# Weights packed by the host in tile order, and one ring of six 8 KB buffers for weights and modulations, in a seven-part network on one core

## The chip, the cores and the metric

The kernel runs on one core of one Trainium2 chip. The metric is the device time of one execution in microseconds. What the host does to the inputs before the launch is not in it. Three runs of the kernel before took 1244.87, 1247.49 and 1250.49 us (median 1247.49).

## The reference

The reference is a network on `x` of 256 tokens by 1024 features, in float32, with seven parts in a row: mixer ab, feed-forward, mixer cd, feed-forward (the first block), feed-forward, convolution and state space mixer, feed-forward (the second block). Cut to the frame:

```python
def first_block(...):
    for layer in range(2):
        shift, scale, gate = split(c @ mod_w[layer, 0] + mod_b[layer, 0], 3)
        h = rms_norm(x, norm_w[layer, 0, 0]) * (1 + scale) + shift
        y = mixer_ab(h, ...) if layer % 2 == 0 else mixer_cd(h, ...)
        x = x + gate * rms_norm(y, norm_w[layer, 0, 1])
        ... # the same with swiglu(h, ffn_w_in[layer], ffn_w_out[layer])
def swiglu(h, w_in, w_out):
    gate, up = split(h @ w_in, 2)
    return (silu(gate) * up) @ w_out          # 1024 -> 2 x 2816 -> 1024
```

Each mixer is a projection of `h` by a matrix of 1024 rows, attention in several kinds over heads of 64 features (in the second block a short convolution and a state space model), and an output projection of 1024 by 1024. Each part needs three modulation vectors of 1024 (shift, scale, gate), each a product of one condition vector with a matrix of 1024 by 1024; that makes 21, the first two of which are made at the start.

## The kernel before, in words

**Products.** A float32 product is made of three passes (`mm3`, L106 to L108): a weight tile that has come from DRAM as `raw` is split by ScalarE into a high part (`whi`, L184) and by VectorE into a low part (`wlo`, L185), each in a ring of four tiles. Where the other operand is one piece, the raw tile goes to TensorE as it is (L104, L447). TensorE's order is the program's; the other engines and the DMA issues are ordered by a scheduler that simulates the timeline. All loads are issued by SP, one after the other: an issue that has to wait for its buffer holds those behind it.

**Weights.** `raw()` gives tiles of 8 KB per partition in a ring of four. `load_cols` (L198) takes columns of a matrix of 1024 rows: for 256 columns it is one load of 1 MB in rows of 1 KB, for pairs of 128 columns two loads of 512 KB in rows of 512 B. `load_rows` (L206) takes 512 rows. `tok_items` (L783) loads `ab_v`, three column ranges for each of two halves, so six loads. `load_q` (L721) loads the queries of the two groups apart. `loads_perm` (L941) loads the output weights of the two attention mixers in the order of the heads: two loads of 64 partitions each for one tile, rows of 4 KB. The feed-forward part (`ffn`) takes a step per 256 columns of gate and up (two tiles, four splits), then eleven tiles of the down matrix (L587). A mixer's `finish` calls `ahead`, which loads the first weights of the part that follows.

**Modulations.** `mod_start` clears an accumulator (POOL, L242), loads the bias into its first row (4 KB, L243), and then in eight pieces loads 1024 numbers per partition (`mraw`, 4 KB rows, a ring of four of its own, L250) and adds them, scaled, on VectorE (L252). `mod_end` sums over the partitions with two products (L276, L277). This work is queued in the background (`bg`, `pay`) and called between the steps of each part, for a later part.

```python
r = self.wp.tile([128, D], F32, tag="mraw", name="mraw", bufs=4)
nc.sync.dma_start(out=r, in_=wv[:, kk, :])
with self.behind(kk == 0):
    nc.vector.scalar_tensor_tensor(acc, r, c[:, kk:kk + 1], acc, ALU.mult, ALU.add)
```

**The first two modulations** (`start`, L1612) come in loads of 512 KB, rows of 2 KB, in quarters, summed on TensorE (L1616) and VectorE (L1619).

**Small loads.** The relative bias is written to DRAM (`rd`) and read back as tiles T, four loads of 32 partitions each (`bias_load`, L828); in the first mixer the copy out of T at L1016 comes before the softmax of later heads (L611, L618) on VectorE. The position embeddings (`setup`, L1695) are turned by TensorE at L1697. L1003 spreads the compressed values.

**Order in time** in the profile: start to some 40 us, mixer ab to 187, feed-forward to 384, mixer cd to 513, feed-forward to 714 and 905, the third mixer to 1049, the last feed-forward to the end.

Of the kernel before, what the change touches and what calls it, by code (L numbers as in the profile page):

```python
# [27 lines left out]
# per part of the network: weight tiles kept split beyond the ring's, modulations made early (and where),  # L28
# budgets and lags of the background work, parts with a second accumulator
# [4 lines left out]
ACC2 = (1, 3, 4)  # L34
E_F32 = 2.7182817459106445
# [3 lines left out]
def shape_constants(np):  # L39
# [20 lines left out]
    return c, oh, m  # L60


class Net:
# [74 lines left out]
    def plan(self, slots):  # L138
        """the waiting work, by its time, over steps of the given slack"""
# [51 lines left out]
    def load_cols(self, w, cols):  # L191
        """[1024, n] columns (a list of (start, stop)) -> raw [128, 8, total]"""
        tot = sum(b - a for a, b in cols)
        r = self.raw()
        v = r[:, :8 * tot].rearrange("p (k n) -> p k n", k=8)
        o = 0
        for a, b in cols:
            self.nc.sync.dma_start(out=v[:, :, o:o + b - a],  # L198
                                   in_=w[:, a:b].rearrange("(k p) n -> p k n", p=128))
            o += b - a  # L200
        return v

    def load_rows(self, w, r0, c0, c1):
        """rows r0 .. r0 + 511 of some columns -> raw [128, 4, n]"""
        r = self.raw()[:, :4 * (c1 - c0)].rearrange("p (k n) -> p k n", k=4)
        self.nc.sync.dma_start(out=r, in_=w[r0:r0 + 512, c0:c1].rearrange("(k p) n -> p k n", p=128))  # L206
        return r
# [6 lines left out]
    def chain(items, ahead=1):  # L214
        """items (prepare, run): closures that prepare `ahead` items beyond their own"""
# [9 lines left out]
    def proj_a(self, w, xh, xl):  # L225
        """weights [128, 8, 128] stationary -> psum [128 features, 256 tokens]"""
# [6 lines left out]
    # ---------------------------------------------------------------- mods  # L233
    def mod_start(self, w, b, c, grain):
        """b + c @ w, as partial sums over 128 partitions"""
# [7 lines left out]
        nc.sync.dma_start(out=acc[0:1, :], in_=b)  # L243
        wv = w.rearrange("(p k) n -> p k n", p=128)

        def piece(i):
# [7 lines left out]
        return acc, [piece(i) for i in range(8 // grain)]  # L254

    def behind(self, on):
        """behind the last part's norm on the vector engine"""
# [12 lines left out]
    def mod_end(self, b, part, kind, arg, dst):  # L270
        """sum over partitions, for all partitions: dst [128, 1024]"""
# [13 lines left out]
    def mod(self, key, w, b, c, kind, arg, row=None, grain=2):  # L285
        """queue the work on one modulation vector; the result is self.m[key]"""
        box = {}

        def start():
            box["acc"], box["pieces"] = self.mod_start(w, b, c, grain)  # L290
# [46 lines left out]
    def mean_sq(self, srcs, n):  # L337
        """two halves of rows [128, 512] -> their parts of the mean square"""
# [6 lines left out]
    def norm_ew(self, h, ws, sh):  # L345
        """token-major rms_norm(x) * ws + sh, rows of half h: two tiles of 512 columns"""
# [13 lines left out]
    def norm_tr(self, h, ts, hh, hl):  # L360
        """into feature-major hi and lo parts"""
# [12 lines left out]
    def post_norm(self, h, ys, gw):  # L374
        """x += rms_norm(y) * gw, rows of half h"""
# [17 lines left out]
    def boundary(self, s):  # L393
        """what follows the output projection of part s: -> ew(h, ys), tr(h)"""
# [43 lines left out]
    # ---------------------------------------------------------------- dense  # L438
# [14 lines left out]
    def out_items(self, ys, halves, loads, ks, nk, xh, xl, keep=None, pool=None):  # L453
        """items for two k-tiles each; loads(i, raw) fills raw [128, 2, 1024] with the rows of two k-tiles"""
        def prepare(i):
            r = self.raw().rearrange("p (k n) -> p k n", k=2)
            loads(i, r)
# [28 lines left out]
    def ahead(self, n=2):  # L486
        """the next part's first weights; self.first() is to hand them over"""
        s, I = self.s + 1, self.I
        if s == 5:
            us = [self.load_cols(I["w_in_2"][0], [(1536 + 256 * i, 1792 + 256 * i)]) for i in range(2)]  # L490
            self.first = lambda: us
        elif s == 2:
            rs = [self.load_rows(I["w_in_cd"][0], 512 * i, 1792, 2304) for i in range(2)]
            self.split_ahead([(r[:, 2 * i:2 * i + 2, :], [2, 512]) for r in rs for i in range(2)], n)
        elif s < 7:
            rs = [self.load_cols(w, [(0, 256)]) for w in self.ffn_weights(s)[:2]]
# [11 lines left out]
    def ffn_weights(self, s):  # L508
        I = self.I
        if s < 4:  # L510
            w = I["ffn_w_in"][s // 2]
            return w[:, :DFF], w[:, DFF:], I["ffn_w_out"][s // 2]
        n = "ffn1" if s == 4 else "ffn2"
        return I[n + "_w_gate_2"][0], I[n + "_w_up_2"][0], I[n + "_w_down_2"][0]

    def out_halves(self, loads, nk, xh, xl, s):
        """the output projection, the last four k-tiles half of the rows after half"""
# [3 lines left out]
        items = self.out_items(ys, (0, 1), loads, range(joint), nk, xh, xl)  # L521
        items += self.out_items(ys, (0,), loads, range(joint, nk // 2), nk, xh, xl, kept, self.fp)
# [21 lines left out]
    def ffn(self, s, wg, wu, wd, hh, hl):  # L544
        nc = self.nc
        with self.tc.tile_pool(name="ffn", bufs=1) as fp:
# [10 lines left out]
            # the first columns token-major: half 0 before half 1 is there  # L557
# [13 lines left out]
            for c in range(1, NF // 2):  # L571
                rg = self.load_cols(wg, [(256 * c, 256 * c + 256)])
                ru = self.load_cols(wu, [(256 * c, 256 * c + 256)])
                for j in range(2):
# [9 lines left out]
                    self.pay(WP)  # L584

            def loads(i, r):
# [1229 lines left out]
```

## Time and profile before

| | |
|---|---|
| median of three runs | 1247.49 us |
| span of the profiled execution | 1248.2 us |
| mean granted TensorE clock in it | 0.980 |
| TensorE busy | 1177.6 us |
| VectorE busy | 919.5 us |
| ScalarE busy | 611.5 us |
| moved by DMA | 304.38 MB, 244 GB/s |
| share of the 16 DMA engines | 74.7% |

The span runs from the first to the last instruction of the execution that was profiled; the page has no other time of that execution. A busy time is the union of an engine's instructions. In the rows, "x4" says that four instructions were merged, and what stands in square brackets or behind the bar is the engine's idle time before, with the instruction or load that ended it. The DMA share of a stretch is a mean over the 16 engines; it can come out a little over 1. The granted clock is 1 at 2.4 GHz and 0.5 at 1.2 GHz.

### The profile page before, as it was taken

What the parts mean: (1) busy time and instruction counts of PE and PEld (TensorE: products, weight loads), DVE (VectorE), ACT (ScalarE), POOL (GpSimd) and SP (SyncE); (2) the same over time, 40 slices, a digit from 0 to 9 for tenths busy, and PEclk for the clock granted to TensorE, in tenths of its full rate; (3) what the DMA queues carried; (4) which work ended last, traced back from release to release, by engine and by line L of the source; (5) the groups of instructions that cost most, each with busy time, mean ns of one, the idle gap of its engine ahead of it and who ended that gap; (6) DMA issues with size and microseconds to landing.
All of it is one profiled execution on the core that took longest, in us unless ns stands there. A gap on an engine that the chain in (4) does not pass through costs nothing.

```text
span 1248.2 us, 19610 instructions
## 1 busy us (share of the span) xinstructions
PE 1177.6 (94%) x7475; PEld 1019.2 (82%) x7475; DVE 919.5 (74%) x1378; ACT 611.5 (49%) x1110; POOL 136.9 (11%) x182
## 2 busy tenths in 40 slices
PE   6897999999999969899999989999999979999997
PEld 2795658999887955699998789998888747999986
DVE  6786839877758677796985699789559978755545
ACT  2364635445444645454454546776642423544433
POOL 2000000000001003100100010000007951000000
PEclk9997999999999989999999999999999989999999
DMA  9999498968965979798887479789665465755540
GB/s 341 309 277 274 121 283 277 355 211 298 349 227 154 271 242 232 247 342 296 295 314 264 161 242 353 244 314 364 230 201 152 154 211 168 227 165 183 203 169 34
DMA packets 203629, 304.38 MB, mean 244 GB/s; under 512 B 18423, under 2 KB 153331, under 8 KB 203534
## 3 DMA queue, kind: packets, MB, share of 16 engines
q1 hardware_dynamic: 203534, 303.12, 74.7%
q8 instruction: 59, 0.97, 0.3%
q14 instruction: 36, 0.29, 0.1%
HBM read 295.97 MB, written 7.11 MB: 243 GB/s over the span
## 4 chain that ended last, share of the span: by engine, by line
PE 35%; issue 17%; DVE 6%; POOL 3%; ACT 2%; DMA 1%; POOLq 0%; SPq 0%; DVEq 0%; ACTq 0%
PE ps L108 6%; PE ps L106 6%; PE ps L107 6%; PE y L451 3%; PE y L449 3%; PE y L450 3%; PE y L447 2%; PE tok L480 1%; PE ps L1360 1%; DVE st L1412 1%; DVE wlo L185 1%; PE glu L1529 1%; POOL xt L1404 1%; DVE ue L1080 1%; PE ps L365 1%
## 5 line engine op out<-in xcount | busy, mean ns | idle before, releaser
L184 ACT ACTIVATE whi<-raw 128x1024 fp32r<-128x1024 f32 (+2 forms) x308 | 318.4, 1042 | 398.5 <-PE ps L107 158.2
L185 DVE TENSOR_TENSOR wlo<-raw,whi 128x1024 fp32r<-128x1024 f32 (+2 forms) x308 | 368.6, 1204 | 179.1 <-ACT whi L184 178.4
L106 PE MATMUL ps<-hhi,whi 128*128 128x256 f32 x1488 | 424.7, 285 | 1.5 <-DVE st L611 1.5
L108 PE MATMUL ps<-hhi,wlo 128*128 128x256 f32 x1488 | 422.3, 284 | 4.0 <-DVE wlo L185 4.0
L107 PE MATMUL ps<-hlo,whi 128*128 128x256 f32 x1488 | 421.9, 284 | 0.0
L108 PEld LDWEIGHTS ps<-hhi,wlo 128*128 128x128 f32 x1488 | 286.3, 192 | 5.1 <-DVE wlo L185 5.1
L106 PEld LDWEIGHTS ps<-hhi,whi 128*128 128x128 f32 x1488 | 286.3, 192 | 4.2 <-DVE st L611 1.7
L107 PEld LDWEIGHTS ps<-hlo,whi 128*128 128x128 f32 x1488 | 286.4, 192 | 1.4 <-DVE wlo L185 0.5
L252 DVE SCALAR_TENSOR_TENSOR macc<-mraw,c,macc 128x1024 f32<-128x1024 f32 x152 | 194.4, 1280 | 19.4 <-DMA mraw<-in_mod_w_dram 8.5
L449 PE MATMUL y<-whi,gh 128*128 128x512 f32 x352 | 139.7, 397 | 0.0
L450 PE MATMUL y<-wlo,gh 128*128 128x512 f32 x352 | 138.9, 395 | 0.0
L451 PE MATMUL y<-whi,gl 128*128 128x512 f32 x352 | 138.9, 395 | 0.0
L242 POOL MEMSET macc<- 128x1024 f32 x19 | 18.3, 962 | 557.6 <-DVE mlo L267 540.7
L451 PEld LDWEIGHTS y<-whi,gl 128*128 128x128 f32 x352 | 66.1, 188 | 15.8
L450 PEld LDWEIGHTS y<-wlo,gh 128*128 128x128 f32 x352 | 66.2, 188 | 15.4
L449 PEld LDWEIGHTS y<-whi,gh 128*128 128x128 f32 x352 | 66.1, 188 | 15.2
L447 PE MATMUL y<-raw,o 128*128 128x512 f32 x128 | 57.4, 596 | 0.7 <-ACT o L113 0.7
L332 POOL TENSOR_SCALAR ms<-ss 128x1 f32<-128x1 f32 x24 | 11.6, 482 | 372.8 <-ACT junk L342 368.9
L555 DVE TENSOR_TENSOR g<-sg,ps 128x256 f32<-128x256 f32 x80 | 33.3, 416 | 23.0 <-PE ps L108 22.5
L447 PEld LDWEIGHTS y<-raw,o 128*128 128x128 f32 x128 | 23.4, 190 | 27.3 <-issue 25.6
L104 PE MATMUL ps<-h,raw 128*128 128x256 f32 x192 | 43.7, 382 | 1.8 <-DVE cvt L1490 1.8
L618 ACT ACTIVATE p<-p,st 128x128 f32<-128x128 f32 (+1 forms) x64 | 28.4, 444 | 30.3 <-DVE st L611 24.6
(335 smaller groups left out, 1505.5 us busy)
## 6 DMA issues: line engine op xcount, KB each, us to landing
raw<-in_ffn_w_in_dram SPq DMA_DIRECT2D x44, 1024.0 KB
mraw<-in_mod_w_dram SPq DMA_DIRECT2D x80, 512.0 KB
mraw<-in_w_mod_dram SPq DMA_DIRECT2D x72, 512.0 KB
raw<-in_ffn_w_out_dram SPq DMA_DIRECT2D x22, 1024.0 KB
raw<-in_ffn_w_gate_dram SPq DMA_DIRECT2D x22, 1024.0 KB
raw<-in_ffn_w_up_dram SPq DMA_DIRECT2D x22, 1024.0 KB
raw<-in_ffn_w_down_dram SPq DMA_DIRECT2D x22, 1024.0 KB
raw<-in_w_out_ab_dram SPq DMA_DIRECT2D x16, 512.0 KB
```

What stands on the lines that cost most here:

```text
L104: mm(out, lh, rh, start=first, stop=last)
L106: mm(out, lh, rh, start=first, stop=False)
L107: mm(out, lh, rl, start=False, stop=False)
L108: mm(out, ll, rh, start=False, stop=last)
L184: self.nc.scalar.activation(hv, src, AF.Copy)
L185: self.nc.vector.tensor_tensor(lv, src, hv.bitcast(F32), ALU.subtract)
L252: nc.vector.scalar_tensor_tensor(acc, r, c[:, kk:kk + 1], acc, ALU.mult, ALU.add)
L447: mm(ys[h][b], xh[:, k, c], wh[:, 0, sl], start=first, stop=last)
L449: mm(ys[h][b], xh[:, k, c], wh[:, 0, sl], start=first, stop=False)
L450: mm(ys[h][b], xh[:, k, c], wl[:, 0, sl], start=False, stop=False)
L451: mm(ys[h][b], xl[:, k, c], wh[:, 0, sl], start=False, stop=last)
L555: nc.vector.tensor_tensor(g, sg, pu, ALU.mult)
```

## The change

The host lays out every weight matrix as its tiles lie on the chip (`packed`): a tile is a block of DRAM in which each partition's numbers stand in one row, 8 KB for a full tile. One function, `load`, takes a tile with one DMA of 128 partitions. The ring of `raw` has six tiles; the ring `mraw` is gone, and modulations come through `load` too, two of the eight pieces (1 MB) at a time, from the same ring. The arithmetic is the same. The two kinds of modulations of the start keep their own buffers, in rows of 4 KB. The biases of all modulations lie in one array. The compression weights, T and the tables of the state space stay as they are.

```diff
+RING = 6
...
+def packed(np, I):
...
+    def cols(w, *idx):
+        w = w if not idx else np.concatenate([w[:, i] for i in idx], 1)
+        return w.reshape(8, 128, -1).transpose(1, 0, 2)
+    def tiles(w, idx, each):
+        c = np.stack([cols(w, idx[i:i + 128]) for i in range(0, len(idx), 128)])
+        return c.reshape(-1, each, 128, 8, 128).transpose(0, 2, 1, 3, 4)
+    def rows(w, n):
+        return w.reshape(n, -1, 128, w.shape[1]).transpose(0, 2, 1, 3)
...
+    o["ab_v"] = rows(ab[:, np.concatenate([r(896, 1024), r(1152, 1304), r(1944, 2072)])], 2)
+    o["ab_qa"] = tiles(ab, heads, 2)
+    o["ab_out"] = rows(I["w_out_ab"][0][np.concatenate([heads, 512 + heads])], 4)
...
+    o["mod"] = np.stack([m.reshape(128, 4, 2, D).transpose(1, 0, 2, 3) for m in mods[2:]])
...
     def raw(self):
-        return self.wp.tile([128, 2048], F32, tag="raw", name="raw", bufs=4)
+        return self.wp.tile([128, 2048], F32, tag="raw", name="raw", bufs=RING)
...
-    def load_cols(self, w, cols):
...
-    def load_rows(self, w, r0, c0, c1):
...
+    def load(self, src):
+        n = src.shape[1:]
+        r = self.raw()[:, :math.prod(n)]
...
+        self.nc.sync.dma_start(out=v, in_=src)
         return v
...
-                for kk in range(grain * i, grain * i + grain):
-                    r = self.wp.tile([128, D], F32, tag="mraw", name="mraw", bufs=4)
-                    nc.sync.dma_start(out=r, in_=wv[:, kk, :])
+                for kk in range(grain * j, grain * j + grain):
+                    if kk % 2 == 0:
+                        box["r"] = self.load(self.I["mod"][i - 2, kk // 2])
                     with self.behind(kk == 0):
-                        nc.vector.scalar_tensor_tensor(acc, r, c[:, kk:kk + 1], acc, ALU.mult, ALU.add)
+                        nc.vector.scalar_tensor_tensor(acc, box["r"][:, kk % 2], c[:, kk:kk + 1], acc, ALU.mult, ALU.add)
...
-                rg = self.load_cols(wg, [(256 * c, 256 * c + 256)])
-                ru = self.load_cols(wu, [(256 * c, 256 * c + 256)])
+                rg, ru = self.load(wg[c]), self.load(wu[c])
...
-    def loads_perm(self, w, perm):
...
-            if base in perm:
-                for g in range(2):
-                    a = base + 256 * g + 64 * t0
-                    nc.sync.dma_start(out=r[64 * g:64 * g + 64], in_=w[a:a + 128, :].rearrange("(t d) n -> d t n", d=64))
...
-        nk = 4
+        n, nk = w.shape[3], w.shape[2]
         nk2 = min(nk, 1024 // n)
...
-                        nc.sync.dma_start(out=pairs[k // 2], in_=w[:, kk:kk + 2, a:a + 512])
+                        nc.sync.dma_start(out=pairs[k // 2], in_=w[:, k:k + 2])
```

## Rows read from the trace of the kernel before

**Rows 1.** The page: its head, TensorE in 40 slices, and the DMA packets.

```profile
span 1248.2 us, 19610 instructions
...
PE 1177.6 (94%) x7475; PEld 1019.2 (82%) x7475; DVE 919.5 (74%) x1378; ACT 611.5 (49%) x1110; POOL 136.9 (11%) x182
...
PE   6897999999999969899999989999999979999997
...
DMA packets 203629, 304.38 MB, mean 244 GB/s; under 512 B 18423, under 2 KB 153331, under 8 KB 203534
```

**Rows 2.** Stretches: length, busy us of each engine, granted clock, DMA share, GB/s.

```profile
0.00:29.00 29.00, 18.28 (x37) 6.17 (x37) 16.62 (x27) 8.97 (x18) 6.60 (x13) 0.96 0.94 338
...
60.70:98.30 37.60, 36.82 (x285) 34.72 (x283) 29.16 (x98) 24.01 (x65) 0.95 (x1) 1.00 1.11 272
98.30:126.00 27.70, 19.91 (x86) 13.54 (x86) 16.49 (x50) 10.69 (x38) 0.00 (x0) 0.75 1.01 281
...
207.00:384.00 177.00, 177.00 (x1222) 164.82 (x1220) 133.47 (x152) 83.93 (x122) 3.93 (x6) 1.00 0.81 280
405.00:433.00 28.00, 28.00 (x241) 27.42 (x240) 21.02 (x43) 17.00 (x39) 0.96 (x1) 1.00 1.05 277
433.00:463.50 30.50, 21.10 (x140) 17.54 (x140) 18.77 (x38) 12.51 (x33) 0.95 (x1) 0.83 0.83 257
...
1063.00:1216.00 153.00, 153.00 (x1123) 145.87 (x1124) 88.23 (x104) 70.68 (x98) 0.00 (x0) 1.00 0.57 190
```

**Rows 3.** Stretches chosen by the kind of load, same columns.

```profile
98.00:106.00 8.00, 8.00 (x47) 6.51 (x47) 0.00 (x0) 1.79 (x3) 0.00 (x0) 0.79 1.07 225
428.00:440.00 12.00, 12.00 (x100) 11.28 (x99) 4.05 (x10) 7.21 (x17) 0.00 (x0) 1.00 1.05 214
312.00:343.00 31.00, 31.00 (x176) 27.00 (x175) 23.48 (x25) 13.30 (x16) 0.00 (x0) 1.00 0.93 352
```

**Rows 4.** Timeline, first mixer, SP, VectorE and TensorE: start, us, instruction [idle before].

```profile
88.50 2.78 SPq L941 DMA_DIRECT2D raw<-in_w_out_ab_dram  x4
91.38 3.77 SPq L828 DMA_DIRECT2D T<-rd  x4
...
106.50 0.21 DVE L1016 COPY tcb<-T 128x60 f32<-128x60 f32 x1 [8.74 <-DMA T<-rd]
...
112.27 0.66 PE L1003 MATMUL ps<-iddup,zr 128*128 128x64 f32 x2 [5.60 <-DVE zr L1001]
```

**Rows 5.** Timeline, second mixer, SP, VectorE and TensorE.

```profile
428.20 0.40 SPq L243 DMA_DIRECT2D macc<-in_mod_b_dram  x1
...
440.61 1.28 DVE L252 SCALAR_TENSOR_TENSOR macc<-mraw,c,macc 128x1024 f32<-128x1024 f32 x1 [7.36 <-DMA macc<-in_mod_b_dram]
...
458.38 0.80 PE L276 MATMUL ps<-mhi,ones_r 128*128 128x512 f32 x1 [7.94 <-ACT mhi L266]
```

**Rows 6.** Timeline, SP and TensorE before the position embeddings.

```profile
37.33 12.81 SPq L783 DMA_DIRECT2D raw<-in_w_in_ab_dram  x6
...
55.78 0.18 PE L1697 MATMUL ps<-c,pe 32*64 32x32 f32 x1 [2.75 <-DMA mraw<-in_mod_w_dram]
```

**Rows 7.** Timeline where the mixers hand over: ScalarE, then TensorE at both places.

```profile
182.99 2.00 ACT L184 ACTIVATE whi<-raw 128x1024 fp32r<-128x1024 f32 x2 [9.11 <-DMA raw<-in_ffn_w_in_dram]
...
195.41 1.23 PE L365 MATMUL ps<-c,ht 128*128 128x128 f32 x8 [1.93 <-DVE ht L357]
...
523.44 1.23 PE L365 MATMUL ps<-c,ht 128*128 128x128 f32 x8 [3.54 <-DVE ht L357]
```

**Rows 8.** Timeline, third mixer, ScalarE.

```profile
993.34 2.00 ACT L184 ACTIVATE whi<-raw 128x1024 fp32r<-128x1024 f32 x2 [3.05 <-DMA raw<-in_w_out_dram]
```

**Rows 9.** Groups of the page (busy us, mean ns, idle before), and SP's waits.

```profile
L252 DVE SCALAR_TENSOR_TENSOR macc<-mraw,c,macc 128x1024 f32<-128x1024 f32 x152 | 194.4, 1280 | 19.4 <-DMA mraw<-in_mod_w_dram 8.5
...
L108 PEld LDWEIGHTS ps<-hhi,wlo 128*128 128x128 f32 x1488 | 286.3, 192 | 5.1 <-DVE wlo L185 5.1
...
SPq L250 <- DVE macc L252: 118.7, 67, 8.2
```

More of the change, by code (lines that the diff above doesn't have):

```diff
@@ L283, in mod_end, with mod @@
             nc.scalar.activation(dst[:, sl], ps, AF.Copy, scale=float(arg))
-    def mod(self, key, w, b, c, kind, arg, row=None, grain=2):
+    def mod(self, key, i, c, kind, arg, row=None, grain=2):
         box = {}
         def start():
-            box["acc"], box["pieces"] = self.mod_start(w, b, c, grain)
+            box["acc"], box["pieces"] = self.mod_start(i, c, grain)
             if kind in ("ws", "gw"):
@@ L451, in out_step, with out_items @@
                 mm(ys[h][b], xl[:, k, c], wh[:, 0, sl], start=False, stop=last)
-    def out_items(self, ys, halves, loads, ks, nk, xh, xl, keep=None, pool=None):
+    def out_items(self, ys, halves, w, ks, nk, xh, xl, keep=None, pool=None):
         def prepare(i):
-            r = self.raw().rearrange("p (k n) -> p k n", k=2)
-            loads(i, r)
+            r = self.load(w[i])
             return [self.weights(r[:, k:k + 1, :], [1, 1024], xl, pool if 2 * i + k >= nk - self.nextra else None) for k in range(2)]
@@ L508, in ffn_weights, with out_halves @@
     def ffn_weights(self, s):
[L509 to L516, printed above, removed]
+        n = (1, 3, 4, 6).index(s)
+        return [self.I[f"ffn_{x}{n}"] for x in "gud"]
+    def out_halves(self, wd, nk, xh, xl, s):
         ew, tr = self.boundary(s)
@@ L584, in ffn @@
                     self.pay(WP)
-            def loads(i, r):
-                nc.sync.dma_start(out=r, in_=wd[256 * i:256 * i + 256, :].rearrange("(k p) n -> p k n", p=128))
-            self.out_halves(loads, NF, gh, gl, s)
+            self.out_halves(wd, NF, gh, gl, s)
     def scores(self, qt, qs, ks, banks=None):
@@ L754, in q_halves, with a_items @@
         return prepare, run
-    def a_items(self, w, cols, hh, hl, put):
+    def a_items(self, w, hh, hl, put):
         box = {}
+        each = w.shape[2]
         def prepare(n):
-            if n % 2 == 0:
-                box["v"] = self.load_cols(w, [(a, a + 128) for a in cols[n:n + 2]])
-            return self.weights(box["v"][:, :, 128 * (n % 2):128 * (n % 2) + 128], [8, 128], hl)
+            if n % each == 0:
+                box["v"] = self.load(w[n // each])
+            return self.weights(box["v"][:, n % each], [8, 128], hl)
         def run(n, ws):
@@ L767, in run, with tok_items @@
             self.bg()
-        return [(lambda n=n: prepare(n), lambda ws, n=n: run(n, ws)) for n in range(len(cols))]
-    def tok_items(self, w, cols, hh, hl, v, extra=None):
-        n = sum(b - a for a, b in cols)
-        nk = 4
+        return [(lambda n=n: prepare(n), lambda ws, n=n: run(n, ws)) for n in range(each * w.shape[0])]
+    def tok_items(self, w, hh, hl, v, extra=None):
+        n, nk = w.shape[3], w.shape[2]
         nk2 = min(nk, 1024 // n)
@@ L778, in prepare @@
             if k0 % nk == 0:
-                r = self.raw()[:, :nk * n].rearrange("p (k n) -> p k n", k=nk)
-                box["r"] = r
-                o = 0
-                for a, b in cols:
-                    self.nc.sync.dma_start(out=r[:, :, o:o + b - a],
-                                           in_=w[128 * k0:128 * (k0 + nk), a:b].rearrange("(k p) n -> p k n", p=128))
-                    o += b - a
+                box["r"] = self.load(w[k0 // nk])
             k1 = k0 % nk
@@ L906, in mixer_ab @@
             self.cmp_box = box
-            loads = self.loads_perm(I["w_out_ab"][0], (0, 512))
+            loads = I["ab_out"]
             ya, yb = {}, {}
@@ L1513, in end @@
                     into_x(h, ys[h], cst["r"])
-                return self.chain(self.out_items(ys, (h,), loads(0), range(2), 4, ch, None)) + [end]
+                return self.chain(self.out_items(ys, (h,), I["s5_out"], range(2), 4, ch, None)) + [end]
             gl = {}
             def glu_load():
-                gl["w"] = []
-                for i in range(2):
-                    t = self.wp.tile([128, D], F32, tag="mraw", name="gluw", bufs=4).rearrange("p (k n) -> p k n", k=2)
-                    nc.sync.dma_start(out=t, in_=I["glu_w_2"][0, 256 * i:256 * i + 256, :].rearrange("(k p) n -> p k n", p=128))
-                    gl["w"] += [t[:, 0], t[:, 1]]
+                w = self.load(I["s5_glu"][0])
+                gl["w"] = [w[:, k] for k in range(4)]
             def glu(k):
@@ L1529, in glu @@
                     nc.tensor.matmul(gl[f], gl["w"][k][:, 128 * f:128 * f + 128], yg[:, k, :], start=k == 0, stop=k == 3)
-            cols = [c0 + 128 * f for f in range(4) for c0 in (512, 1024, 0)]
-            fill = self.spread(self.chain(self.a_items(w, cols, hh, hl, conv)), 0, 15)
+            fill = self.spread(self.chain(self.a_items(I["s5_c"], hh, hl, conv)), 0, 15)
             c0, c1 = conv_out(0), conv_out(1)
@@ L1560, in mixer_s5 @@
             ys, kept = {}, []
-            for f in self.chain(self.out_items(ys, (0,), loads(512), range(2), 4, *sh, kept)):
+            for f in self.chain(self.out_items(ys, (0,), I["s5_out"][2:4], range(2), 4, *sh, kept)):
                 f()
@@ L1799, in add @@
         I[name] = nc.dram_tensor(f"in_{name}_dram", a.shape, F32, kind="ExternalInput").ap()
+    inputs = {k: np.asarray(v) for k, v in inputs.items()}
     for name in _INS:
         add(name, np.ascontiguousarray(inputs[name]))
+    for name, a in packed(np, inputs).items():
+        add(name, np.ascontiguousarray(a))
     for name, a in zip(("consts", "onehot", "bandmask"), shape_constants(np)):
```

169 lines of the change are left out of this document (76 added, 93 removed).

## The prediction

> **What bounds the kernel now.** The first view to read is the head of the page. TensorE is busy 1177.6 us of the 1248.2 us span, 94%, and in the 40 slices most digits are 9 [rows 1]. The few low digits are what a faster load could repair, so the second view is the table of stretches. In the feed-forward parts TensorE has no idle time at all: 177.00 of 177 us and 153.00 of 153 us, at the full granted clock (1.00, the 2.4 GHz level), while the DMA engines are busy 0.81 and 0.57 of the time [rows 2]. Loads that come faster give nothing there. The table shows two other kinds of stretch. From 60.7 to 98.3 us and from 405 to 433 us the DMA share is 1.11 and 1.05, full, yet only 272 and 277 GB/s are moved. Right behind these, from 98.3 to 126 and from 433 to 463.5 us, TensorE is busy only 19.91 of 27.7 us and 21.10 of 30.5 us, and its granted clock averages 0.75 and 0.83, that is, part of the time it stands at the 1.2 GHz level [rows 2].
>
> The third view, stretches chosen for the kind of load, says why a full DMA moves so little. From 98 to 106 us and from 428 to 440 us, where the output weights of the mixers come in loads of 64 partitions, the share is 1.07 and 1.05 and the rate 225 and 214 GB/s; from 312 to 343 us, where rows of 4 KB go to 128 partitions, a share of 0.93 gives 352 GB/s [rows 3]. Three packets in four are under 2 KB: 153,331 of 203,629 [rows 1].
>
> The fourth view, the timeline by engine, shows what the backlog does. In the first mixer the bias tile T is issued from 91.38 us, behind four such half loads; VectorE, which works in order, stands at the copy out of T for 8.74 us until 106.50 us, and TensorE is then idle 5.60 us before L1003 [rows 4]. In the second mixer the 4 KB bias row of a modulation is issued at 428.20 us and VectorE stands 7.36 us for it until 440.61 us; softmax, behind it in VectorE's order, is late, and TensorE is idle 7.94 us before L276 [rows 5]. In both places a small load waits some 12 us in the DMA queue, not for its own bytes.
>
> **The change part by part, against the profiled span of 1248.2 us** (it lies 0.7 us above the median of the runs, 1247.49).
>
> A, *first modulations*, rows of 2 KB become 4 KB. The first 29 us move at 338 GB/s and share 0.94 [rows 2], 360 at full share; rows of 4 KB gave 352 at 0.93 [rows 3], 378 at full. The gain is 29 x (1 - 360/378) = 1.4 us, at least 0, at most 29 x (1 - 338/378) = 3.1. I take 1.
>
> B, *six loads of `ab_v` become two*. They hold SP's queue from 37.33 us for 12.81 us; the small load of the position embeddings, behind them, is late and TensorE idles 2.75 us before L1697 [rows 6]. Between 0 and 2.75; I take 2.
>
> C, *first mixer*: columns in rows of 512 B and half loads become whole loads. No row shows rows of 8 KB; the nearest are those of 4 KB, so I price them at 352 GB/s, with 378 as upper end and, as lower, today's rate. The 37.6 us at 272 GB/s are 10.2 MB, 29.1 us at 352: 8.5 us earlier. The 8 us at 225 are 1.8 MB, 5.1 us: 2.9 more. Together 11.4 exceed the 8.74 us that VectorE waits, so T should be there in time. TensorE gets back its 5.60 us; the clock can add up to 19.91 x 0.25 = 5.0. Bounds 0 and 10.6; I take 6, since what is late next, the softmax chain on VectorE and ScalarE, follows closely.
>
> D, *second mixer*, the same: 28 us at 277 GB/s are 7.8 MB, 22.0 us at 352, 6.0 us earlier; the part from 433 to 440 at 214 GB/s is 1.5 MB, 4.3 us instead of 7, 2.7 more. 8.7 exceed 7.36. Bounds 0 and 7.94 + 21.10 x 0.17 = 11.5; I take 8, the shift of VectorE and a little of the clock.
>
> By the Trainium skill (DMA: Bandwidth & Descriptors, section Rules for kernel authors) two transfers to the two partition halves use the same engines and just follow each other, so joining them would save nothing; the rows with 214 and 225 against 352 GB/s say otherwise, and I go by them. By that rule C and D would lose the 2.9 and 2.7 us of the half loads and still nearly cover both waits.
>
> E, *ring of six*. At the two places where a mixer hands over to a feed-forward part, ScalarE idles 9.11 us until the first weights land, then VectorE's splits fall among the steps of the norm, and TensorE waits 1.93 us there and 3.54 us at the other place [rows 7]. A tile six loads back is free earlier than one four back. Bounds 0 and 5.5; I take 4.
>
> F, *third mixer*: ScalarE idles 3.05 us for the output weights [rows 8]; the earlier slot saves 0 to 3.05. VectorE is nearly full around it, so I take 1.
>
> G, *modulations in the shared ring*: 152 loads of 512 KB become 76 of 1 MB, and the SP instructions and their waits halve. VectorE idled 19.4 us before 152 pieces, 8.5 of it for DMA, and SP waited 118.7 us for VectorE to free these tiles [rows 9], so loads stand ready ahead of their use. Cost taken: 0; what covers it is that lead, and if it is gone the price is the third rival's. The splits, the matmuls and their order on TensorE stay; `cd_vc` has one split of 1024 columns instead of two of 512, and VectorE and ScalarE may be ordered anew by the scheduler: both at 0, between -2 and +2 us.
>
> Sum: 1 + 2 + 6 + 8 + 4 + 1 = 22 us: 1226.2 for the span, 1225.5 as a median. All upper ends together are 36.5 us.
>
> **The rivals.**
>
> *Only the halves count* (1236 us). Rows of 512 B are perhaps as good as long ones, and the 272 to 277 GB/s come from other traffic in these stretches: the table loads and the half loads themselves. Then C keeps 2.9 us of its queue and D 2.7, A nothing, and with B, E and F (7 us) the gain is about 12. For it: the rows don't separate the sizes. Against: from 60.7 to 98.3 us the share is full at 272 GB/s and the half loads are only its last part. The Trainium skill (same page, section Specifications) puts the least transfer for line rate at 512 B, which would make this rival true for all rows of the weights.
>
> *The queue fills again* (1246 us, from 1240 to 1251). The ring lets SP run six loads of 1 MB ahead, and a small load issued behind them waits up to 6 x 1.05 MB at 352 GB/s = 17.9 us, against 12.4 now (428.20 to 440.61 us) [rows 5]. Then T and the bias row are as late as now. With C and D gone 8 us are left, 1240; with 5.5 us more of waiting at each of both places, 1251. For it: both stretches show a full queue today, and nothing in the change puts small loads first. Against: the tiles are freed by VectorE and TensorE at their old pace, and each MB leaves sooner.
>
> *Modulations hold up the weights* (1268 us, slower). The first piece of each modulation now needs 1 MB landed instead of 512 KB: 3.0 us instead of 1.5 at 352 GB/s. VectorE stands in order at it, the low halves of the weights behind it, and TensorE in a part where it has no slack [rows 2]. There are 152 / 8 = 19 modulations: 19 x 1.5 = 28 us, less the 8 us of A, B, E and F: +20. It decides as soon as VectorE's idle time before L252 grows beyond what the splits are ahead of TensorE; today TensorE's weight loads wait only 5.1 us in all for low halves [rows 9], which speaks against it. A modulation tile waiting for its accumulator also keeps a slot that weights could use.
>
> **How the numbers follow.** Forecast 0.64; only the halves 0.10; the queue fills again 0.15; slower 0.11. This kernel's measurement can tell 0.5%, 6.2 us, from no change: faster is under 1241.3. The first two cases lie there, and 0.03 of the third: 0.77. The rest of the third is within 0.5%: 0.12. Slower: 0.11. The range goes from all upper ends (1211) less half the spread of the three runs (2.8), 1208, up to 1246, the middle of the third case; it leaves out the slower case and half of the third, 0.19. The forecast's own range is 1211 to 1240.
>
> **What would show it.** Right: under the same full share the mixers' stretches move 340 GB/s or more, or the share falls under 0.9; VectorE's 8.74 us before L1016's copy and 7.36 us before the first modulation piece shrink under 3; TensorE's gaps of 5.60 and 7.94 us with them; the clock of these stretches rises above 0.9; the feed-forward stretches keep their lengths within 1 us. Wrong: a wait for T or for a bias row as long as now with a full queue (the second rival), feed-forward stretches that grow, with waits on the low halves or before the modulation pieces (the third), or rates that stay under 300 GB/s where rows were short (the first).

## The result: 1234.4 us, a gain of 13.7 us

| | before | changed |
|---|---|---|
| median of four runs, us | 1248.02 | 1234.36 |
| lowest to highest, us | 1244.87 to 1250.49 | 1233.44 to 1234.67 |
| ratio, 95% interval | | 0.9896 [0.9878, 0.9914] |
| profiled execution and its span, us | [rows 1] | 1234.67, 1232.2 |

The prediction's 1225.5 us was 9 us too low; the result lies in the range, and in the forecast's own one. That the sum came near is in part luck: it took the packing for too little, and the cost of the shared ring, as large as the whole gain, for nothing, as the experiments show.

The page of the changed kernel, head and packets, beside [rows 1]:

```profile
span 1232.2 us, 19361 instructions
...
PE 1176.0 (95%) x7475; PEld 1020.5 (83%) x7475; DVE 921.3 (75%) x1377; ACT 611.0 (50%) x1109; POOL 136.6 (11%) x182
...
DMA packets 62857, 304.33 MB, mean 247 GB/s; under 512 B 16663, under 2 KB 20499, under 8 KB 30382
```

The work is the same, and it moves in 62,857 packets instead of 203,629. The mean rate hardly rises, since the bytes are the same and the span is only 1.3% shorter. The stretches of the mixers, changed kernel, beside [rows 2] (length, busy us of each engine, granted clock, DMA share, GB/s):

```profile
57.30:95.00 37.70, 33.03 (x208) 30.39 (x207) 27.64 (x86) 18.60 (x47) 0.00 (x0) 0.85 0.97 323
95.00:126.00 31.00, 30.21 (x190) 24.45 (x188) 24.04 (x83) 19.20 (x68) 0.99 (x1) 0.94 0.60 229
...
433.00:463.50 30.50, 30.50 (x192) 22.72 (x189) 26.85 (x50) 20.42 (x54) 4.65 (x7) 1.00 0.62 218
```

The second mixer is healed: from 433 to 463.5 us TensorE is busy 30.50 of 30.5 us at clock 1.00. In the first, the hole has moved: from 57.3 to 95 us TensorE, which before was nearly full there, now lacks 4.7 us and part of its clock. The start of the same matmul in three traces shows where the time went (the spans of the first two differ by 16.0 us, the medians by 13.7, so a gain read here can be up to 2.3 us too large); the third is the best of the experiments, every weight packed but the rings as they were (`e9_mods_512k` below):

| matmul (line before / after) | before | changed | packed, old rings |
|---|---|---|---|
| position embeddings, L1697 / L1679 | 55.78 | 55.00 | 55.41 |
| first transposed probabilities, L636 / L676 | 81.76 | 85.26 | 80.42 |
| the 25th of them | 125.71 | 122.70 | 114.02 |
| first hand-over, L365 / L414 | 195.41 | 191.86 | 182.27 |
| second mixer's first scores, L600 / L640 | 422.94 | 417.37 | 407.79 |
| its last value products, L1096 / L1093 | 497.61 | 480.87 | 471.33 |
| third mixer's first states, L104 / L158 | 950.78 | 933.43 | 923.96 |
| its sums of squares, L1459 / L1452 | 1010.71 | 993.91 | 980.69 |
| last product, L451 / L500 | 1240.28 | 1224.17 | 1211.07 |

Against the kernel before, the changed kernel gains 11.2 us in the second mixer (it is 5.6 ahead at its first row and 16.7 at its last), 3.0 by the 25th transposed block of the first, after a loss of 3.5 on the way, and nothing in the third. Against the packing with the old rings it is 4.8 us behind at the first transposed block, 8.7 at the 25th, 9.6 at the hand-over, no more than that up to the third mixer, and 13.2 behind that mixer's sums of squares. Its timeline in the first mixer (start, us, instruction [idle before]; SP, ScalarE and TensorE):

```profile
47.98 13.58 SPq L841 DMA_DIRECT2D T<-rd  x12
61.71 0.35 SPq L255 DMA_DIRECT2D raw<-in_ab_qa_dram  x1
...
76.39 1.06 ACT L238 ACTIVATE whi<-raw 128x1024 fp32r<-128x1024 f32 x1 [2.94 <-DMA raw<-in_ab_qa_dram]
...
85.26 0.33 PE L676 MATMUL ps<-c,p 128*128 128x128 f32 x1 [3.44 <-ACT p L667]
...
92.27 1.96 SPq L841 DMA_DIRECT2D T<-rd  x4
...
106.17 0.82 SPq L255 DMA_DIRECT2D raw<-in_ab_out_dram  x2
```

Two things stand here that the prediction did not have. SP issues the second T, at 92.27 us, *ahead* of the output weights at 106.17; before, four half loads went ahead of it [rows 4]. And the query weights are issued at 61.71 us, behind twelve loads of T on which SP stands for 13.58 us; ScalarE, in order, waits for them, its exponentials come late, and TensorE idles 3.44 us. The clock adds to it: behind this gap the changed kernel has a granted clock of 0.50, with TensorE busy all the time, where the packing with the old rings has 1.00 (the two in this order):

```profile
88.00:92.00 4.00, 4.00 (x19) 2.83 (x18) 2.95 (x13) 0.35 (x1) 0.00 (x0) 0.50 0.95 352
```

```profile
88.00:92.00 4.00, 4.00 (x29) 3.38 (x28) 2.01 (x12) 3.79 (x16) 0.00 (x0) 1.00 0.94 332
```

The second mixer has the same new order:

```profile
427.25 0.26 SPq L292 DMA_DIRECT2D macc<-in_mod_bias_dram  x1
427.96 0.33 SPq L255 DMA_DIRECT2D raw<-in_cd_out_dram  x1
```

The bias row now leaves ahead of the output weights; before, they went ahead of it [rows 5]. So two explanations of the vanished stalls were open: the loads are faster, or the shared ring has put them in another order.

### The profile page after: what moved, and what is told of

It is laid out like the page before. It is cut to its first block, busy times and chain, and to the rows that moved or that the text cites. A ratio compares the mean times of both kernels' runs of the same rounds, so it can differ in the third digit from the quotient of the medians.

```text
span 1232.2 us, 19361 instructions
## 1 busy us (share of the span) xinstructions
PE 1176.0 (95%) x7475; PEld 1020.5 (83%) x7475; DVE 921.3 (75%) x1377; ACT 611.0 (50%) x1109; POOL 136.6 (11%) x182
## 2 busy tenths in 40 slices
DMA packets 62857, 304.33 MB, mean 247 GB/s; under 512 B 16663, under 2 KB 20499, under 8 KB 30382
## 4 chain that ended last, share of the span: by engine, by line
PE 62%; issue 17%; DVE 8%; DMA 6%; POOL 4%; ACT 2%; POOLq 0%; SPq 0%; DVEq 0%; ACTq 0%
PE ps L162 11%; PE ps L160 11%; PE ps L161 11%; PE y L500 5%; PE y L498 5%; PE y L499 5%; PE y L496 4%; PE tok L528 2%; DMA raw<-in_ab_cmp_dram 1%; PE ps L640 1%; PE o L684 1%; DVE wlo L239 1%; PE ps L1353 1%; DMA T<-rd 1%; DVE st L1405 1%
## 5 line engine op out<-in xcount | busy, mean ns | idle before, releaser
L301 DVE SCALAR_TENSOR_TENSOR macc<-raw,c,macc 128x1024 f32<-128x1024 f32 x152 | 195.1, 1283 | 7.3 <-DMA raw<-in_mod_dram 3.5
L500 PE MATMUL y<-whi,gl 128*128 128x512 f32 x352 | 138.9, 395 | 0.0
L500 PEld LDWEIGHTS y<-whi,gl 128*128 128x128 f32 x352 | 66.1, 188 | 15.8
L599 DVE TENSOR_TENSOR g<-sg,ps 128x256 f32<-128x256 f32 x80 | 33.5, 418 | 25.6 <-PE ps L162 25.2
L158 PE MATMUL ps<-h,raw 128*128 128x256 f32 x192 | 45.9, 396 | 5.0 <-DVE cvt L1483 5.0
L158 PEld LDWEIGHTS ps<-h,raw 128*128 128x128 f32 x192 | 37.5, 198 | 11.2 <-DVE cvt L1483 5.2
L496 PEld LDWEIGHTS y<-raw,o 128*128 128x128 f32 x128 | 23.4, 190 | 28.0 <-issue 25.6
```

Of the source, the lines that this page charges most:

```text
L301: nc.vector.scalar_tensor_tensor(acc, box["r"][:, kk % 2], c[:, kk:kk + 1], acc, ALU.mult, ALU.add)
L496: mm(ys[h][b], xh[:, k, c], wh[:, 0, sl], start=first, stop=last)
L500: mm(ys[h][b], xl[:, k, c], wh[:, 0, sl], start=False, stop=last)
L599: nc.vector.tensor_tensor(g, sg, pu, ALU.mult)
```

## Experiments

All times are medians, each against the kernel before on the same chip (1246.5 to 1247.6 us).

| | rings (weights + modulations) | what is not packed | us |
|---|---|---|---|
| before | 4 x 8 KB + 4 x 4 KB | all | 1246.5 to 1248.0 |
| `e10_whole_out` | 4 x 8 KB + 4 x 4 KB | all but mixers' output weights | 1234.6 |
| `e13_ffn_rows` | 4 x 8 KB + 4 x 4 KB | feed-forward | 1222.1 |
| `e9_mods_512k` | 4 x 8 KB + 4 x 4 KB | nothing | **1220.9** |
| `e11_ring5` | 5 x 8 KB + 2 x 4 KB | nothing | 1248.7 |
| `e3_two_rings` | 4 x 8 KB + 2 x 8 KB | nothing | 1228.9 |
| `e7_rings_halves` | 4 x 8 KB + 2 x 8 KB | output weights in halves | 1239.0 |
| `e8_rings_short` | 4 x 8 KB + 2 x 8 KB | attention's column tiles | 1233.5 |
| changed kernel | 6 x 8 KB shared | nothing | 1234.4 |
| `e12_mod_pieces` | 6 x 8 KB shared | modulations by 512 KB | 1234.4 |
| `e5_t_later` | 6 x 8 KB shared | nothing; T emitted later | 1233.2 |
| `e2_short_rows` | 6 x 8 KB shared | column tiles | 1234.4 |
| `e1_halves` | 6 x 8 KB shared | output weights in halves | 1250.8 |
| `e6_ring_only` | 6 x 8 KB shared | all | 1258.2 |

**Speed or order: half loads in the one ring.** `parts` is 2 for the output weights of the attention mixers:

```diff
-        self.nc.sync.dma_start(out=v, in_=src)
+        for g in range(parts):
+            sl = slice(128 // parts * g, 128 // parts * (g + 1))
+            self.nc.sync.dma_start(out=v[sl], in_=src[sl])
```

> The changed kernel, but each load of the attention mixers' output weights is split again into two of 64 partitions (8 KB rows stay). Two theories of where the 13.7 us came from. SPEED (the forecast's): each load lands sooner, so T and the bias row wait less; the halves at 214 to 225 GB/s were 2.9 and 2.7 us of the two queues, so 3 to 6 us of the gain come back: 1237 to 1240 us, and TensorE gets an idle stretch again before the pooled keys' product or before the modulation sums. ORDER: in the shared ring SP issues the output weights behind T and behind the bias row, so their speed is out of the way: 1234 us within 1.5, no idle stretch over 1 us at those two places.

1250.8 us, ratio 1.0029 [1.0011, 1.0047]: the whole gain is gone, and both theories missed. ORDER was right that nothing happens at T and at the bias row. The loss is elsewhere, in the bursts of output weights ahead of the two hand-overs. The stretch from 150 to 166 us, changed kernel, then this one:

```profile
150.00:166.00 16.00, 16.00 (x58) 8.69 (x57) 5.45 (x14) 5.80 (x14) 0.00 (x0) 1.00 0.80 324
```

```profile
150.00:166.00 16.00, 16.00 (x64) 9.06 (x62) 5.30 (x11) 5.57 (x12) 1.82 (x3) 1.00 1.02 229
```

And this kernel's timeline, SP, ScalarE, TensorE:

```profile
147.26 4.76 SPq L257 DMA_DIRECT2D raw<-in_ab_out_dram  x6
156.56 0.33 SPq L257 DMA_DIRECT2D raw<-in_ffn_g_dram  x1
...
172.82 2.00 ACT L238 ACTIVATE whi<-raw 128x1024 fp32r<-128x1024 f32 x2 [9.02 <-DMA raw<-in_ffn_g_dram]
...
176.58 2.08 PE L498 MATMUL y<-raw,o 128*128 128x512 f32 x2 [10.49 <-ACT o L167]
```

The same bytes at 229 GB/s with full engines, instead of 324 at a share of 0.80. The first feed-forward weights land behind them; ScalarE stands for these 9.02 us, in order, and the copy of o that TensorE needs is queued behind: 10.49 us idle, where the changed kernel had 1.36. Ahead of the second hand-over it is the same: ScalarE stands 11.34 us, and TensorE is idle 6.59 us before L416. With one ring the output weights are issued late, so their rate decides.

**Short rows in the one ring.** The tiles of 128 columns lie k-major (`transpose(0, 1, 3, 2, 4)` in `tiles`).

> The changed kernel, but the tiles of 128 columns (projections of all three mixers) lie in DRAM k-major again, so that their loads have pieces of 512 B; one load of 1 MB per tile as before. SPEED: from 57 to 95 us and from 400 to 433 us the DMA is full at about 275 GB/s again, T and the bias row are up to 8 us later, and 6 to 14 us come back: 1240 to 1248 us, 1243 the likeliest. ORDER: the rate of these stretches falls, but the order of issue stays, and there are several us of slack in both places: 1234 to 1237 us.

1234.4 us, ratio 0.9895 [0.9871, 0.9918], as ORDER said. It is a weak test: its page counts 17,819 packets of 2 to 8 KB (9,883 in the changed kernel) and hardly more of under 2 KB, so these loads did not move in packets of 512 B.

**Two rings, all packed.**

```diff
-RING = 6
+RING = 4
...
-                        box["r"] = self.load(self.I["mod"][i - 2, kk // 2])
+                        r = self.wp.tile([128, 2048], F32, tag="mraw", name="mraw", bufs=2)
+                        box["r"] = self.load(self.I["mod"][i - 2, kk // 2], r)
```

> The changed kernel with every weight packed, but a ring of four for weights and one of two 8 KB tiles for modulations, as much memory as the ring of six. SP then issues two output weight loads ahead of T and two ahead of the bias row, as the kernel before did with its half loads. SPEED: the loads are as fast as in the changed kernel, only the hand-overs lose their 3 us: 1234 to 1238 us. ORDER: T and the bias row wait behind 2.1 MB of output weights, 6 us at 352 GB/s, plus what lies ahead of these; VectorE stands for T and for the bias row again, TensorE idles over 3 us in at least one of the two mixers: 1240 to 1248 us.

1228.9 us, 0.9842 [0.9810, 0.9874]: ORDER falls as the only cause, and the shared ring is found to cost. SP again issues two output loads ahead of T and of the bias row, as before, yet TensorE's gaps of 5.60 and 7.94 us [rows 4, 5] don't come back.

**The one ring, nothing packed.** The kernel before with `bufs=6`, 1 MB modulations in the ring, and in it too the small weights of the third mixer (`gluw`) that had used the modulations' buffers.

> The kernel before, no weight packed (512 B, 1 KB and 2 KB rows, half loads), but weights and modulations in one ring of six 8 KB tiles, modulations in loads of 1 MB. SPEED: the full queue at 272 GB/s stays, T and the bias row are as late as before, only the hand-overs gain: 1243 to 1249 us. ORDER: SP issues T and the bias row ahead of the output weights, both stalls go without any packing: 1233 to 1238 us, and VectorE's waits for T and for the bias row are under 3 us.

1258.2 us, 1.0078 [1.0052, 1.0104]: slower than before by 11.5 us, where SPEED had it at the old time and ORDER at a gain. Yet its order does to TensorE's stalls most of what ORDER said, with nothing packed, though VectorE still waits 4.5 us for T (SP, then TensorE):

```profile
96.81 1.90 SPq L831 DMA_DIRECT2D T<-rd  x4
110.41 2.69 SPq L944 DMA_DIRECT2D raw<-in_w_out_ab_dram  x4
...
184.41 2.07 PE L450 MATMUL y<-raw,o 128*128 128x512 f32 x2 [10.94 <-ACT o L113]
...
463.31 0.80 PE L279 MATMUL ps<-mhi,ones_r 128*128 128x512 f32 x1 [3.55 <-ACT mhi L269]
```

T leaves ahead of the output weights and the stall of 5.60 us [rows 4] is gone; the one of 7.94 us [rows 5] is down to 3.55. So faster loads (`e3_two_rings`) and the new order are each enough for the first, and both help the second. What this kernel loses lies elsewhere: it has the gap of the half loads in one ring, 10.94 us at the output projection, 6.60 us before the position embeddings, and the two losses of the shared ring that are shown below. So the ring alone is a loss.

**Halves and short rows in two rings.** The edits of the first two runs, on `e3_two_rings`, whose order of issue on SP they leave alone; the short column tiles now in loads of 512 KB.

> The kernel of the two rings (1228.9 us), its order of issue unchanged, but each load of the attention mixers' output weights split into two of 64 partitions. HALVES (whole loads are what the packing is worth): four half loads stand ahead of T and four ahead of the bias row, 2.1 MB each time at about 229 GB/s (9.2 us) instead of 340 (6.2 us), so both are 3 us later, and the bursts of output weights ahead of the hand-overs take a third longer; the one ring lost 16.4 us by the same edit, but had its output weights issued later: here 1234 to 1244 us, 1238 the likeliest, with TensorE idle before the pooled keys or the modulation sums. ROWS (the length of the rows is what it is worth): 1228 to 1231 us.

> The kernel of the two rings, its order of issue unchanged, but the attention mixers' tiles of 128 columns lie k-major in DRAM and come in loads of 512 KB with packets of 512 B (the earlier run with 1 MB loads of such tiles moved packets of 2 KB). HALVES: the queue of small rows is fuller from 57 to 95 us and from 400 to 433 us, but the output weights behind it are fast: 1228 to 1232 us. ROWS: packets of 512 B ran at 31 ns in the kernel before, 264 GB/s, so 4 MB before T and 5 MB before the bias row take 4 to 5 us longer, and TensorE waits for both: 1233 to 1242 us.

The halves: 1239.0 us, 10.1 more than `e3_two_rings`, as HALVES expected, and TensorE idles 2.45 us before L1003, the place of the T stall, and 2.82 before the modulation sums. From 88 to 106 us, first with whole loads, then with halves:

```profile
88.00:106.00 18.00, 18.00 (x117) 15.16 (x116) 12.95 (x43) 12.17 (x46) 0.95 (x1) 0.91 0.90 307
```

```profile
88.00:106.00 18.00, 15.55 (x115) 13.71 (x114) 10.89 (x36) 9.42 (x34) 0.95 (x1) 1.00 1.03 223
```

The loads of output weights differ in nothing but their partitions: 307 against 223 GB/s, the lower rate at the fuller share. The records of single packets in the two traces agree: a packet of 8 KB that starts in this stretch takes 352 ns on the mean with whole loads and 592 with halves. The Trainium skill (DMA: Bandwidth & Descriptors, section Rules for kernel authors) advises one transfer of 128 partitions in place of two halves; these runs agree, and give the price, which its reason (the two follow each other on the same engines) would not have led one to expect. The short rows: 1233.5 us, between 1225.9 and 1234.8, against 1223.5 to 1230.9: the two overlap, and neither theory is settled by it.

**The packing alone.** Against the changed kernel, cut:

```diff
-RING = 6
+RING, MODS = 4, 4
...
-                    if kk % 2 == 0:
-                        box["r"] = self.load(self.I["mod"][i - 2, kk // 2])
+                    r = self.wp.tile([128, D], F32, tag="mraw", name="mraw", bufs=MODS)
+                    self.load(self.I["mod"][i - 2, kk // 2][:, kk % 2], r)
```

> Every weight packed, and the two rings of the kernel before exactly: four 8 KB tiles for weights, four 4 KB tiles for modulations, which come in loads of 512 KB. This is the packing alone. If the size of the modulations' loads is of no account: 1226 to 1232 us, as with two 8 KB tiles. If the forecast's third rival has some truth (a first piece needs 1 MB landed), it is faster, 1222 to 1226. If loads of 1 MB carried part of the gain (fewer instructions and waits on SP): 1233 to 1240.

1220.9 us, 0.9796 [0.9765, 0.9827]: 25.6 us faster than before and 13.5 faster than the change. It is faster than any of the three cases said. Where the 8 us against `e3_two_rings` may come from, the row of the modulations tells (VectorE, same columns as [rows 9]). Here, in `e3_two_rings`, and in `e11_ring5`, a later run with two 4 KB tiles:

```profile
L301 DVE SCALAR_TENSOR_TENSOR macc<-mraw,c,macc 128x1024 f32<-128x1024 f32 x152 | 195.1, 1284 | 4.3 <-DMA mraw<-in_mod_dram 2.3
```

```profile
L302 DVE SCALAR_TENSOR_TENSOR macc<-mraw,c,macc 128x1024 f32<-128x1024 f32 x152 | 194.4, 1279 | 12.5 <-DMA mraw<-in_mod_dram 9.7
```

```profile
L301 DVE SCALAR_TENSOR_TENSOR macc<-mraw,c,macc 128x1024 f32<-128x1024 f32 x152 | 196.6, 1293 | 61.0 <-DMA mraw<-in_mod_dram 57.2
```

With two tiles instead of four VectorE waits longer: 12.5 us in place of 4.3 with tiles of 8 KB (as many bytes ahead, in fewer loads), 61.0 with tiles of 4 KB (half the bytes ahead). So the bytes that are fetched ahead count for more than the number of tiles. VectorE's 8.2 us of added waits in `e3_two_rings` are as many as the kernel lost; that TensorE lost them for these waits was not shown.

**Where the shared ring loses.** Two repairs were tried on the changed kernel: T emitted a slot later, and modulations in two loads per tile.

> The changed kernel with its one ring of six, but the last four of the twelve loads of T (for the heads of the second softmax) are emitted a slot later, so that SP issues the first query tile ahead of them. REORDER (the ring's 7 us loss at 62 to 85 us is the place of the T loads ahead of the query tiles on SP): the query tile lands 3 to 5 us earlier, the exps behind its split on ScalarE too: 1227 to 1231 us, idle time of TensorE at 82 us under 1.5. SLOT (the query tiles are late for want of a free tile of the shared ring, or the eight loads of T before them suffice): 1233 to 1236 us.

> The changed kernel, one ring of six, but each modulation tile of 8 KB is filled by two loads of 512 KB instead of one of 1 MB; tiles and ring unchanged. GRAIN (the shared ring is slow because the first piece of a modulation needs 1 MB landed and VectorE stands for it): 1224 to 1229 us. SHARING (a modulation holds a tile that a weight load needs, and SP, in order, stands or issues other things first): 1232 to 1236 us.

Neither helped: 1233.2 and 1234.4 us, and TensorE's gap at the first transposed block is 8.00 and 7.50 us. GRAIN falls. REORDER was not put to the test: moving four of the T loads brought the query tile's issue only from 61.71 to 60.94 us, since SP stood at the other eight, as SLOT allowed for. Both results lie where SLOT and SHARING said. What differs is seen beside the trace of the packing alone: SP in the first mixer, then TensorE and the third load of output weights in the third:

```profile
49.78 0.44 SPq L255 DMA_DIRECT2D raw<-in_ab_qa_dram  x1
52.26 15.49 SPq L841 DMA_DIRECT2D T<-rd  x12
...
959.70 2.62 PE L158 MATMUL ps<-h,raw 128*128 128x256 f32 x7 [1.76 <-DVE cvt L1483]
...
970.13 0.42 SPq L255 DMA_DIRECT2D raw<-in_s_out_dram  x1
```

With a ring of their own the first query weights leave at 49.78 us, ahead of T; in the shared ring they stand behind T, at 61.71. All fourteen kernels divide at this point. In the six with the one ring the first query load follows the T loads (eight of them in `e5_t_later`) and is issued at 60.9 to 64.5 us, and the first transposed block starts at 85.1 to 90.4; in the eight others it goes ahead of T, at 47.2 to 57.5, and the block starts at 78.4 to 81.9. With nothing packed there is one kernel on each side, the kernel before and `e6_ring_only`, so this loss does not hang on the packing. Whether the query load lacks a tile that a modulation holds, or the scheduler places it later for another reason, was not shown. In the third mixer it is the other way round, as the changed kernel shows (SP's third load of output weights, VectorE, TensorE):

```profile
957.55 0.42 SPq L255 DMA_DIRECT2D raw<-in_s_out_dram  x1
...
966.36 1.75 DVE L239 TENSOR_TENSOR wlo<-raw,whi 128x1024 fp32r<-128x1024 f32 x1
...
970.36 1.68 DVE L239 TENSOR_TENSOR wlo<-raw,whi 128x1024 fp32r<-128x1024 f32 x1
971.97 0.41 DVE L1483 TENSOR_TENSOR cvt<-cvt,ps 128x256 f32<-128x256 f32 x1
...
972.43 5.90 PE L158 MATMUL ps<-h,raw 128*128 128x256 f32 x16 [5.01 <-DVE cvt L1483]
```

No modulations are loaded there, the six tiles are all free for weights, and the output weights come earlier: the third load is issued 24.1 us after the mixer's first states (957.55 - 933.43), against 46.2 (970.13 - 923.96). Two splits, 3.4 us, are then put ahead of the step that frees TensorE's bank, and TensorE waits 5.01 us instead of 1.76. This gap of 5.0 us is in all six kernels with the one ring and in none of the others.

**Whole output weights alone, and the deeper ring.** The kernel before with its two attention mixers' output projections fed from packed tiles. Of these sixteen tiles twelve came in half loads before, the other four, in the second mixer, already in whole ones of 1 MB; all sixteen change from rows of 4 KB to 8 KB:

```diff
-            loads = self.loads_perm(I["w_out_ab"][0], (0, 512))
+            loads = lambda i, r: nc.sync.dma_start(out=r, in_=I["ab_out"][i])
```

> The kernel before with one part of the packing alone: the output weights of the two attention mixers as the host's packed tiles, 1 MB to 128 partitions in one load; every other weight in its old short rows, the old two rings, the old order of issue. HALVES ONLY (rows of 512 B to 4 KB are as good as 8 KB in effect): nearly all of what the packing alone gave, 25.6 us, comes from these sixteen tiles: 1221 to 1230 us. ADDITIVE (halves undone cost 10 us in the two rings, the rows the rest): 1234 to 1239 us; the first rival of the prediction said 1236 for its case. ROWS: 1243 or more.

1234.6 us, 0.9895 [0.9868, 0.9921]: ADDITIVE. The sixteen tiles give 13.0 of the 25.6 us. That most of it is the halves follows from `e7_rings_halves`, where halves cost 10.1 us with rows of 8 KB; the part of the longer rows was not run alone. What is left in its trace (VectorE and TensorE, first mixer, then second):

```profile
104.31 0.21 DVE L1016 COPY tcb<-T 128x60 f32<-128x60 f32 x1 [6.19 <-DMA T<-rd]
...
110.09 0.66 PE L1003 MATMUL ps<-iddup,zr 128*128 128x64 f32 x2 [4.99 <-DVE zr L1001]
...
442.72 0.50 PE L276 MATMUL ps<-mhi,ones_r 128*128 128x512 f32 x1 [2.19 <-ACT mhi L266]
```

The bias stall falls from 7.94 us [rows 5] to 2.19 by these tiles alone, in the old order of issue. The T stall stays, 4.99 of 5.60 us [rows 4]: VectorE's wait is 2.6 us shorter, and that is not enough. It needs the rest of the packing as well; with all packed (`e9_mods_512k`), no idle stretch of TensorE over 1 us is left there.

> Every weight packed, a ring of five 8 KB tiles for weights and two 4 KB tiles for modulations, the same memory as four and four. If the depth of the weights' ring is worth something at the hand-overs and the modulations need no more than two tiles: 1214 to 1219 us against 1220.9. If modulations with two tiles fall behind (VectorE waits for each 512 KB load): 1222 to 1235.

1248.7 us, 1.0005 [0.9985, 1.0025], worse than either case: two small tiles for modulations, even with a fifth for weights, cost 27.8 us. Here the chain of the forecast's third rival is seen, at the second hand-over (VectorE, then TensorE):

```profile
530.86 1.28 DVE L301 SCALAR_TENSOR_TENSOR macc<-mraw,c,macc 128x1024 f32<-128x1024 f32 x1 [5.62 <-DMA mraw<-in_mod_dram]
532.06 1.22 DVE L239 TENSOR_TENSOR wlo<-raw,whi 128x1024 fp32r<-128x1024 f32 x1
...
533.33 0.38 PE L162 MATMUL ps<-hhi,wlo 128*128 128x256 f32 x1 [3.33 <-DVE wlo L239]
```

VectorE stands for a modulation piece, the low half of a weight is split behind it, and TensorE waits 3.33 us for that.

> The kernel with every weight packed and the old two rings (1220.9 us), but the feed-forward weights lie in DRAM as before: rows of 1 KB for gate and up, 4 KB for down, one load of 1 MB per tile. The prediction gave the feed-forward parts no gain, since TensorE has no idle time there: 1219 to 1224 us, and the DMA share of these stretches rises. If their shorter loads had shortened the hand-overs, where the first gate and up weights are late: 1224 to 1230.

1222.1 us (1221.4 to 1224.1, against 1218.3 to 1224.3): packing the feed-forward weights changes nothing that can be measured. From 207 to 384 us the DMA share is 0.77 with rows of 1 KB and 0.73 with 8 KB, and TensorE is busy 174.69 us in both.

## Why the prediction came out as it did

The direction was right, and so was the mechanism for the packing, though it was priced too low: alone it gives 25.6 us, against 18 in the sum of 22, in which 4 (E) were put down to the ring. The term that failed is **G**, the modulations in the shared ring, priced at 0 with a cover read from VectorE's idle time and SP's waits. It measured 13.5 us (1234.4 against 1220.9; 12.0 if each is taken against its own runs of the kernel before). The two errors, in opposite directions, brought the sum within 9 us. Its price was looked for in the wrong place: in the landing of the first piece, where `e12_mod_pieces` shows nothing, and in VectorE's waits, which fell from 19.4 us [rows 9] to 7.3 in the changed kernel. The traces place it in the order in which SP issues the loads when one ring gives out all tiles: some 9 us in the first mixer, with the clock that falls there, and some 4 in the third. That is read from the same order in all six kernels with the one ring; no run put the order right inside the shared ring.

- **A and B**, 1 and 2 us: nothing. The position embeddings start 0.8 us earlier, and TensorE still waits 2.45 us for their load.
- **C**, 6 us: with the packing alone the offset goes from 0.4 us at the position embeddings to 11.7 at the 25th transposed block, so 11.3, just over the upper bound of 10.6. In the changed kernel TensorE's stall of 5.60 us went too, but with the later query weights 2.2 are left (0.8 to 3.0).
- **D**, 8 us: 11.2 us in the changed kernel and 11.1 with the packing alone, from the second mixer's first scores to its last value products, near the bound of 11.5. The 8 were hardly more than the stall of 7.94 us. What was sized too small is the clock, which stands at 1.00 from 433 to 463.5 us, against 0.83 [rows 2], and a second gap in the kernel before, 1.46 us at 447.30 us, was left out.
- **E**, 4 us by the ring of six: at the first hand-over the gap of 1.93 us [rows 7] fell to 0.71, at the second 3.54 to 2.81. The packing with the old rings gains there as well (0.78 and 2.99), so the depth of the ring is not its cause, and `e11_ring5` shows what depth taken from the modulations costs.
- **F**, 1 us: -0.6 in the changed kernel (17.4 to 16.8), 3.2 in the packing alone (26.8 to 30.0).

Of the rivals, *Only the halves count* named the right lever with the wrong measure: the output weights, mostly their halves, gave 13.0 us, rows and the rest 12.6. How much of that the short column tiles carry was not separated (`e8_rings_short`). *The queue fills again* did not come: in the changed kernel the new order put the small loads first, and with the old rings, where output weights go ahead of them again, the loads landed soon enough. *Modulations hold up the weights* was right that the ring costs, with half of its 28 us, but not by its way: VectorE does not stand at 1 MB pieces. That way is seen only in `e11_ring5`. Its last sentence, that a modulation keeps a slot which weights could use, may be what delays the query weights of the first mixer; in the third no modulation is loaded, and the loss there comes from weights that arrive too early.

That the shared ring's order would change was not asked at all: "nothing in the change puts small loads first" was wrong. In a kernel whose SP order comes from a scheduler, the number of free tiles is part of the order.

## What to carry to other kernels

Loads to half the partitions are the first thing to mend where short waits stand behind them: here sixteen tiles, twelve of which had come in halves, gave half of what the packing gave. Change layouts and rings in separate steps: here one was worth 25.6 us and the other cost 13.5, and the sum looked like a modest success. Before making a ring shared or deeper, write down the order of issue that results, and ask which load loses its place and which comes too early.

## What was not expected

Half loads of 64 partitions move 223 to 229 GB/s at a DMA share of 1.02 to 1.03, with 8 KB rows too, where whole loads move 307 to 324 at 0.80 to 0.90. Each packet takes longer, 592 ns instead of 352; why was not tried. Rows of 1 KB in the feed-forward parts cost 0.04 of DMA share and no time. And a load that lands earlier can cost time: the output weights of the third mixer, 22 us sooner in the one ring, took VectorE's turn from the step that TensorE waited for.
